# Loading the first image pair by one transfer and the second by four, in a Winograd-row convolution

## The chip, the core and the metric

The kernel runs on one core of a Trainium2 chip. The metric is the device time of one execution in microseconds. The core has five engines that each run their own instructions in order: TensorE (PE; its weight loads are listed apart as PEld), VectorE (DVE), ScalarE (ACT), GpSimd (POOL) and SyncE (SP). SP, ACT and POOL also issue DMA transfers. In the profile a transfer issued on SP is in queue q1, on ACT in q10, on POOL in q0.

## The reference

A 3x3 convolution with zero padding of one, over 16 images of 64 channels and 64x64 pixels, to 128 channels, all in float32:

```python
x_pad = np.pad(x, ((0, 0), (0, 0), (1, 1), (1, 1)), mode='constant')
for b in range(batch):
    for co in range(c_out):
        for ci in range(c_in):
            for kh in range(3):
                for kw in range(3):
                    output[b, co] += weight[co, ci, kh, kw] * x_pad[b, ci, kh:kh+h, kw:kw+w]
```

The input is 16.8 MB, the output 33.6 MB, the weights 0.3 MB.

## The kernel before

Two images make a pair: their 2 x 64 channels fill the 128 partitions, one row of 64 x 64 pixels in each, so that a pair is a block of 128 consecutive rows of `x_rows`. There are eight pairs (`p` from 0 to 7). A matmul takes 64 partitions, one image; those of the two images (`b2`) follow each other on the two halves of the array.

Pairs of output rows share work. With `s` the sum of the input rows 2j and 2j+1 (tile `ss`), the product of the middle kernel row with `s` (tile U) is common to the even and the odd output row. The even row needs U plus two more kernel-row products (A), the odd row U plus two others (B). That is five kernel-row products for two rows instead of six. The combined weights G21 and G01 are made on POOL (lines 86 and 87), after TensorE has turned the weights (line 84) and ScalarE has copied them out (line 85).

A pair is worked in four blocks of eight row pairs. In each block TensorE runs 6 matmuls for U, 12 for A and 12 for B; ScalarE copies U from PSUM to SBUF (`ut`, line 155); VectorE adds it to A (line 164) and to B (line 167) into the output tiles `ots`. PSUM holds eight tiles. A block takes six, so that the A of the next block finds a free one only when the copies of line 155 have freed U's. After the last block of a pair the first image's output goes out on SP's queue (line 171), the second's on ACT's (line 172 puts it in `held`, line 161 issues it in the next block). The last pair's outputs go out in halves.

Pairs 2 to 7 are loaded by POOL (line 58), each by one transfer that casts float32 to float16 on the way. Pairs 2, 3 and 4 are issued at the start, behind line 87; pairs 5 to 7 wait until a buffer of `xpool` is free. Pairs 0 and 1 come as float32 over SP's queue, into two buffers of the output pool, and are cast on the chip:

- line 42: the weights, 288 KB
- lines 45 and 46: pair 0 (`x0`) in two transfers, rows 0 to 17 of every channel and rows 18 to 63
- line 48: pair 1 (`x1`) in one transfer, all 128 partitions

Pair 0 is then summed by VectorE (line 91) and cast by ScalarE (line 92) in four pieces each, the casts by `cuts` at rows 18, 34 and 50. Each piece waits for the transfers that bring its rows. Pair 1 is summed by POOL in two pieces (line 105) and cast by ScalarE in four, two in the third block of pair 0 and two in the fourth (line 159). `keep` holds instructions in the order in which they are written.

Of the kernel before, what the change touches and what calls it, by code (L numbers as in the profile page):

```python
# [13 lines left out]
def kernel(  # L14
# [6 lines left out]
    nc = tc.nc  # L21
# [7 lines left out]
    x_rows = x.rearrange("b c h w -> (b c) h w")  # L29
# [12 lines left out]
    nc.sync.dma_start(w_raw, w_flat)  # L42
    x0 = opool.tile([128, H, W], F32, tag="ot", name="x0")
    cuts = [(0, 18), (18, 34), (34, 50), (50, 64)]
    for lo, hi in ((0, 18), (18, 64)):
        nc.sync.dma_start(x0[:, lo:hi, :], x_rows[0:128, lo:hi, :])  # L46
    x1 = opool.tile([128, H, W], F32, tag="ot", name="x1")
    nc.sync.dma_start(x1, x_rows[128:256, :, :])
    ident = const.tile([128, 128], F16)
    make_identity(nc, ident)  # L50
    w16 = const.tile([CO, CI * 9], F16)
# [50 lines left out]
    for p in range(NP):  # L102
# [8 lines left out]
        for blk in range(4):  # L111
# [57 lines left out]
            if blk in parts:  # L169
                lo, hi = parts[blk]  # L170
# [34 lines left out]
```

## Time and profile before

| | us |
|---|---|
| median of 3 runs (126.14 to 127.47) | 126.81 |
| the profiled execution | 126.72 |
| its span | 124.9 |
| TensorE busy | 106.7 |
| VectorE busy | 82.6 |
| ScalarE busy | 44.4 |
| POOL busy | 36.9 |
| mean of all DMA, GB/s | 356 |

The span is the stretch of the execution that the profile's clock covers; the time of an execution is some 1.8 us longer. TensorE's busy time is modelled, so a high share of it is not yet a proof that it bounds the kernel. The rows by slice cut the span into 40 parts of 3.1 us and give a digit of busy tenths for each. The DMA row is the mean over 16 DMA engines. The DMA rate counts bytes as they are written, so that a transfer that casts to half the size shows half the rate of what it reads. A number of microseconds "to landing" runs from the issue of a transfer to its completion signal.

The order of the first 24 us, from the timeline: the weights land at 3.4, rows 0 to 17 of pair 0 at 5.9, the first matmul of the convolution starts at 6.59, the other rows land at 9.5, pair 1 lands at 16.9, the matmuls of pair 1 begin at 22.36, and the first store is issued at 23.12.

### The profile page before, as it was taken

The page shows a single profiled execution, that of the slowest core. Times are in us where ns is not written, and L with a number is a line of the kernel's source. Part 1 is how long each engine was busy: PE and PEld are TensorE (multiplying, and loading weights), DVE is VectorE, ACT ScalarE, POOL GpSimd, SP SyncE. Part 2 cuts the span into 40 slices and gives each one's busy share as a digit, 9 for nine tenths or more (in the row PEclk, how much of TensorE's full clock was granted, in tenths as well). Part 3 has the DMA queues.
Part 4 walks back from the last instruction along what each step waited for, and adds up shares of the span by engine and source line. Part 5 has one row for each costly group of instructions (what it writes and reads, how often), then busy time and mean ns, then how long its engine had stood idle before and what let it go on. Part 6 is the DMA issues. An engine that isn't in the chain of part 4 may idle for free.

```text
span 124.9 us, 2407 instructions
## 1 busy us (share of the span) xinstructions
PE 106.7 (85%) x978; PEld 55.9 (45%) x978; DVE 82.6 (66%) x132; ACT 44.4 (36%) x76; POOL 36.9 (30%) x29
## 2 busy tenths in 40 slices
PE   0489999999999999999999999999999999990000
PEld 0334455555555555555555555555555555540000
DVE  0106897877787778788788878777877787772000
ACT  4439569633333333333333333333333333330000
POOL 2391059997059001760008500093000000000000
PEclk9999999999999999999999999999999999999755
DMA  4999999999999999999999999999999999999991
GB/s 127 341 429 409 289 220 220 210 254 357 386 344 354 328 375 359 367 338 344 386 359 354 338 344 401 428 435 441 414 430 430 425 420 435 435 420 407 430 391 66
DMA packets 4042, 44.48 MB, mean 356 GB/s; under 512 B 448, under 2 KB 448, under 8 KB 704
## 3 DMA queue, kind: packets, MB, share of 16 engines
q1 hardware_dynamic: 1872, 21.27, 41.2%
q10 hardware_dynamic: 1296, 16.78, 31.7%
q0 software_dynamic: 864, 6.29, 24.4%
q8 instruction: 7, 0.11, 0.3%
q14 instruction: 3, 0.02, 0.0%
HBM read 17.07 MB, written 33.55 MB: 405 GB/s over the span
## 4 chain that ended last, share of the span: by engine, by line
PE 78%; DMA 6%; ACT 3%; DVE 1%; SPq 1%; issue 1%; DVEq 0%
PE acc L141 78%; DMA x<-in_x_dram 6%; ACT xs L92 2%; ACT ut L155 1%; DVE ot L164 1%; DVE ot L167 0%; DVEq L200 0%; SPq L46 0%; SPq L42 0%; DVEq L164 0%
## 5 line engine op out<-in xcount | busy, mean ns | idle before, releaser
L141 PE MATMUL acc<-xs,Wt 64*128 64x504 f16 (+3 forms) x768 | 94.8, 378 | 0.2
L141 PEld LDWEIGHTS <-Wt 64*128 64x128 f16 x960 | 54.7, 96 | 51.6 <-issue 4.2
L155 ACT COPY ut<-acc 128x512 f32<-128x512 f32 x64 | 34.3, 589 | 60.3 <-issue 40.6
L164 DVE TENSOR_TENSOR ot<-acc,ut 128x512 f32<-128x512 f32 x64 | 41.2, 686 | 21.9 <-PE acc L141 18.0
L167 DVE TENSOR_TENSOR ot<-acc,ut 128x512 f32<-128x512 f32 x64 | 41.1, 684 | 0.0
L141 PE MATMUL acc<-ss,Wt 64*128 64x504 f16 (+1 forms) x192 | 32.5, 384 | 1.0 <-DVE ss L67 1.0
L67 POOL TENSOR_TENSOR ss<-xs 128x1024 f16<-128x1024 f16 x12 | 25.2, 2126 | 23.6 <-DMA xs<-in_x_dram 12.5
L67 DVE TENSOR_TENSOR ss<-x 128x512 f16<-128x512 f32 x4 | 2.6, 689 | 8.8 <-DMA x<-in_x_dram 8.8
L58 POOL DMA_DIRECT2D xs<-in_x_dram x6 | 3.5, 578 | 13.3 <-PE acc L141 13.3
L67 POOL TENSOR_TENSOR ss<-x 128x1024 f16<-128x1024 f32 x2 | 4.7, 2360 | 7.1 <-DMA x<-in_x_dram 7.1
L84 PE MATMUL wp<-ident,w 128*64 128x128 f16 x18 | 1.3, 328 | 4.3 <-POOL w L52 4.3
L92 ACT CAST xs<-x 128x1024 f16<-128x1024 f32 (+2 forms) x4 | 4.0, 1048 | 2.3 <-DMA x<-in_x_dram 2.3
L159 ACT CAST xs<-x 128x1024 f16<-128x1024 f32 x4 | 4.0, 1058 | 0.0
L84 PEld LDWEIGHTS <-w 128*64 128x64 f16 x18 | 1.1, 210 | 4.2 <-POOL w L52 4.2
L85 ACT CAST Wt<-wp 128x384 f16<-128x384 f32 x3 | 1.2, 487 | 2.9 <-PE wp L84 2.9
L86 POOL TENSOR_TENSOR Wt<-Wt 128x384 f16<-128x384 f16 x1 | 1.5, 1460 | 1.7 <-ACT Wt L85 1.7
L85 ACT ACT_TABLE_LOAD x1 | 1.3, 1283 | 0.7 <-PEq L189 0.7
L52 POOL CAST w<-w_raw 128x576 f16<-128x576 f32 x1 | 0.7, 663 | 2.2 <-DMA w_raw<-in_weight_dram 2.2
L87 POOL TENSOR_TENSOR Wt<-Wt 128x384 f16<-128x384 f16 x1 | 0.9, 902 | 0.0
masks.py:199 POOL TENSOR_SCALAR_AFFINE_SELECT ident<-ident 128x128 f16<-128x128 f16 x1 | 0.3, 292 | 0.1
masks.py:197 POOL MEMSET ident<- 128x128 f16 x1 | 0.2, 205 | 0.3 <-POOLq L189 0.3
L189 POOL MEMSET const-float32-0.0<- 128x1 f32 x1 | 0.1, 98 | 0.2 <-issue 0.2
(3 smaller groups left out, 0.3 us busy)
## 6 DMA issues: line engine op xcount, KB each, us to landing
out_dram<-ot SPq DMA_DIRECT2D x7, 2048.0 KB, 20.1
out_dram<-ot ACTq DMA_DIRECT2D x7, 2048.0 KB, 19.8
xs<-in_x_dram POOLq DMA_DIRECT2D x6, 1024.0 KB, 25.9
x<-in_x_dram SPq DMA_DIRECT2D x1, 2048.0 KB, 14.8
out_dram<-ot SPq DMA_DIRECT2D x2, 1024.0 KB, 11.6
out_dram<-ot ACTq DMA_DIRECT2D x2, 1024.0 KB, 11.5
x<-in_x_dram SPq DMA_DIRECT2D x1, 1472.0 KB, 7.9
x<-in_x_dram SPq DMA_DIRECT2D x1, 576.0 KB, 4.7
```

The costliest lines, as they stand in the source:

```text
L58: keep(nc.gpsimd.dma_start(xs[p], x_rows[128 * p : 128 * p + 128, :, :]))
L67: eng.tensor_add(ss[p][:, lo : lo + n, :], v[:, lo : lo + n, 0, :], v[:, lo : lo + n, 1, :])
L84: nc.tensor.matmul(wp[q : q + 64, k * CO : k * CO + CO], w16[:, t::9], ident)
L85: keep(nc.scalar.copy(wrow(g), wp[:, 0 : 3 * CO]))
L86: keep(nc.gpsimd.tensor_sub(wrow(G21), wrow(G2), wrow(G1)))
L87: keep(nc.gpsimd.tensor_sub(wrow(G01), wrow(G0), wrow(G1)))
L92: keep(nc.scalar.copy(xs[0][:, lo:hi, :], x0[:, lo:hi, :]))
L141: nc.tensor.matmul(tiles[b2][:, lo - j0 : hi - j0, c_lo:c_hi], Wt[p0 : p0 + 64, wi, kw, :], rhs, start=i == 0, stop=i == n - 1,)
L155: keep(nc.scalar.copy(ut, U[b2]))
L159: keep(nc.scalar.copy(xs[1][:, lo : lo + 16, :], x1[:, lo : lo + 16, :]))
L164: nc.vector.tensor_add(ots[b2][:, j0 : j0 + RB, 0, :], A[b2], us[b2])
L167: nc.vector.tensor_add(ots[b2][:, j0 : j0 + RB, 1, :], Bt[b2], us[b2])
```

## The change

Pair 0 is loaded by one transfer of all 64 rows in place of two. Pair 1 is loaded by four transfers of 32 partitions each, of all rows, in place of one. Order on the queue, tiles, and everything that reads them stay as they are; a reader of `x0` now waits for the one transfer, a reader of all partitions of `x1` for four.

```diff
     cuts = [(0, 18), (18, 34), (34, 50), (50, 64)]
-    for lo, hi in ((0, 18), (18, 64)):
-        nc.sync.dma_start(x0[:, lo:hi, :], x_rows[0:128, lo:hi, :])
+    nc.sync.dma_start(x0, x_rows[0:128, :, :])
     x1 = opool.tile([128, H, W], F32, tag="ot", name="x1")
-    nc.sync.dma_start(x1, x_rows[128:256, :, :])
+    for c in range(0, 128, 32):
+        nc.sync.dma_start(x1[c : c + 32, :, :], x_rows[128 + c : 160 + c, :, :])
```

## The prediction, made before the changed kernel ran

> **What bounds the kernel now.** I read the page first: the rows by slice, the DMA queues and the chain.
>
> ```profile
> span 124.9 us, 2407 instructions
> ...
> PEclk9999999999999999999999999999999999999755
> DMA  4999999999999999999999999999999999999991
> ...
> q1 hardware_dynamic: 1872, 21.27, 41.2%
> q10 hardware_dynamic: 1296, 16.78, 31.7%
> q0 software_dynamic: 864, 6.29, 24.4%
> ...
> PE 78%; DMA 6%; ACT 3%; DVE 1%; SPq 1%; issue 1%; DVEq 0%
> ```
>
> The chain says TensorE, 78%. But it ends at the last tensor_add, at 113.3 us, and the span goes on to 124.9: the last 11 us are stores that drain. The three queues' shares add to 97.3% and the DMA row is full from slice 2 to slice 39. So there are two lines side by side: TensorE's from the first matmul on, and a DMA line without a hole. A delay on the first reaches the end only if it makes a hole in the second; work added to the second reaches the end by itself.
>
> Next, the chain in order of time, for what the first pair's load holds up.
>
> ```profile
> 1.63 7.86 DMA x<-in_x_dram
> 9.49 0.02 issue
> 9.51 2.83 ACT xs L92 x3
> 12.34 0.98 ACT ut L155 x2
> 13.32 0.04 issue
> 13.36 97.40 PE acc L141 x882
> ```
>
> Today's path into steady state is not the first matmul (6.59) but rows 18 to 63 of x0: they land at 9.49, ScalarE casts three pieces (2.83), then copies the first U out of PSUM (0.98). In TensorE's weight-load row of the timeline the wait shows as 12.88 to 13.37, 0.49 us.
>
> Last, stretches (start:end, length, busy us of PE, PEld, DVE, ACT, POOL, then clock, DMA share, GB/s) and the DMA issues.
>
> ```profile
> 3.00:4.00 1.00, 0.00 (x0) 0.00 (x0) 0.00 (x0) 0.00 (x0) 0.47 (x1) 1.00 1.00 283
> ...
> 9.00:12.00 3.00, 3.00 (x22) 1.33 (x20) 1.90 (x3) 2.49 (x3) 0.88 (x2) 1.00 1.01 429
> 20.00:24.00 4.00, 4.00 (x42) 2.11 (x38) 2.97 (x5) 3.80 (x6) 4.00 (x3) 1.00 1.02 213
> 100.00:110.00 10.00, 10.00 (x98) 5.28 (x94) 7.95 (x13) 3.57 (x7) 0.00 (x0) 1.00 1.01 431
> ```
> ```profile
> x<-in_x_dram SPq DMA_DIRECT2D x1, 2048.0 KB, 14.8
> ...
> x<-in_x_dram SPq DMA_DIRECT2D x1, 1472.0 KB, 7.9
> x<-in_x_dram SPq DMA_DIRECT2D x1, 576.0 KB, 4.7
> ```
>
> A busy DMA moves 429 GB/s where descriptors are large, 283 where x0's first 18 rows travel, and fills SBUF at 213 where the loads of line 58 cast to half the bytes.
>
> **First pair, one transfer.** The packet records of the trace hold 128 descriptors for each transfer of x. Those of 4608 bytes took 280 ns on average, those of 11776 took 448, those of 16384 took 611. Sixteen engines share them: today 128 x (280 + 448) / 16 = 5.82 us, as one transfer 128 x 611 / 16 = 4.89. The DMA line loses 0.9 us of work. If the slowness of the small ones came from being the first to move and not from their size, it loses nothing: 0 to 0.9. All 64 rows then land between 9.49 - 0.9 = 8.6 and 9.5. One issue of 0.42 us leaves SP's queue.
>
> What this does to TensorE: the first DVE sum waits for rows 0 to 17, which landed at 5.85 (1.16 issued, 4.7 to land); the first matmul came 0.74 later. The same 0.74 after 8.6 to 9.5 gives a first matmul at 9.3 to 10.2, so 2.75 to 3.65 later. From the landing ScalarE has all four casts to do (1.17 + 2.83) and two copies (0.98), 5.0 us; TensorE itself reaches the point where it waited today 0.74 + 6.3 = 7.0 us after the landing. So the 0.49 us wait goes, and TensorE's own work is late next: a shift of 2.26 to 3.16 for everything behind it. Two bounds more. TensorE's weight loads come every 0.43 us from 6.98 to 11.09 and about twice as fast afterwards, although the granted clock says 1.00: it starts slow. That slow stretch is 4.5 us from the first matmul and 6.8 from the transposes at 4.25; starting its count anew could cost (6.8 - 4.5) / 2 = 1.15 more, while a step at a fixed 11.1 us would leave only 1 to 1.8 us of it and give back about 1.4. The shift is 0.9 to 4.3, 2.7 as the value.
>
> How much of it the end sees is read from the stores. Those of the sixth pair were issued at 87.2 and 87.8, and the answer for that stretch reads:
>
> ```profile
> out_dram<-ot SPq DMA_DIRECT2D x1, 2048.0 KB, 17.0
> out_dram<-ot ACTq DMA_DIRECT2D x1, 2048.0 KB, 16.5
> ```
>
> They land at 104.2; with 0.5 us from last packet to landing (as x0: 8.99 and 9.49) DMA has work until 103.7. The next stores are issued at 99.97, and a packet follows 1.0 us (w_raw) to 1.8 us (this store) after its issue: 101.0 to 101.8. The margin is 1.9 to 2.7 us, 2.3 as the value, the smallest at any of the stores: the last ones, 112.78 and 113.37, land 10.9 and 10.6 later though 2 MB at 429 need 4.9. So TensorE's shift of 2.7 alone costs 0.4, and nothing if DMA has more work than today: then the line has no hole.
>
> **Second pair, four transfers of 32 channels.** The same bytes in the same 128 descriptors of 16384, behind x0 on the same queue. SP issues three more at 0.43 us and is done about 3.4 instead of 2.5; the next thing on SP is a store at 23.12, and x1's packets start at 8.4, so this is hidden. POOL's sum (line 67) and ScalarE's cast (line 159) wait on four semaphores for one; the waiting instructions seen on queues take 17 ns each.
>
> The open price is how fast a transfer that lies on a quarter of the partitions moves: every transfer of this trace spans all 128. Lowest: as x1 today, 611 ns, nothing added. (A gain is excluded: 429 GB/s is what every large transfer here gets.) Highest: the slowest that a load fills SBUF here, 213 GB/s, so 2.10 MB in 9.8 us instead of 4.9, +4.9. The row nearest by size is x0's first piece, 576 KB beside these 512: its 4608 bytes at 611/16384 would be 172 ns and took 280, 1.63 times as long. By that ratio x1 costs 4.89 x 0.63 = +3.1, and I take it; both ends stay for the range. It is DMA work, while DMA is full, so nothing hides it.
>
> [...]
>
> Who waits if x1 lands late? At +2.2 (3.1 less 0.9) it lands at 19.1. ScalarE reaches the cast of x1 at 17.61 + 2.26 = 19.9, no wait. At +4.9 it stands 1.9 us, and behind it the fourth block's U copy and so PSUM and TensorE; that adds at most 1.9 to TensorE's shift and falls into DMA's larger backlog. POOL's two sums (2.36 each) end by 23.8, the first at 21.5; the second pair's matmuls begin at 22.36 + 2.26 = 24.6.
>
> **Sum.** DMA work +3.1 - 0.9 = +2.2; TensorE's shift 2.7 is under the margin then, 2.3 + 2.2. The profiled execution took 126.72 (1.8 beside its span), 0.09 under the median of 126.81: 126.72 + 2.2 = 128.9.
>
> **Rivals and chances.** Forecast, 0.62: the quarter transfers are slower, 1.5 to 4.9; with 0 to 0.9 saved, 127.3 to 131.6, likeliest 128.9. For it: the full DMA row. Against: the descriptors are x1's own.
>
> Second, 0.20: the quarters cost nothing, and TensorE's late start makes a hole before the seventh pair's stores. The shift of 2.26 to 4.3 less the margin of 1.9 to 2.7 is 0 to 2.4: 126.7 to 129.1, middle 127.1. For it: the chain. Against: each store but that one has a larger margin.
>
> Third, 0.18, not slower: the quarters cost nothing, and x0's saved work reaches the end. It decides at the margin: with 0.9 less work the margin is 1.4, so the shift must be under 1.4. It is if TensorE speeds up at a fixed time (0.9 to 1.8). Then 126.72 - 0.9 = 125.8; with a shift of 2.3 it is 126.7. Against: the two small descriptors may have been slow for being first.
>
> A difference under 1% (1.27 us) can't be told from none. Slower by more: 0.57 of the first and 0.10 of the second, 0.67. Same: 0.05, 0.10 and 0.13, 0.28. Faster: 0.05, the third with the ramp better than its row. The range 126.1 to 131.0 leaves out some 0.08 at each end.
>
> **What would show it.** x0's single landing at 8.6 to 9.5 and a first matmul 0.74 behind; no 0.49 us gap before the second block's weight loads. x1's packets at 700 to 1200 ns instead of 611, GB/s under 300 around 9 to 12 us, x1's last landing after 18. The DMA row still full up to the drain and the last add 2 to 4 us later, with the last stores landing in about as much or more than 10.6. I am wrong if x1's packets stay at 611, or if the DMA row has holes at 26 or 102 us; then the margin sets the time.

## The result and the profile after

The changed kernel takes 129.71 us at the median of six executions, the kernel before 126.73: a ratio of 1.0239 with a 95% interval of 1.0211 to 1.0267. It is slower by 3.0 us. The profiled execution took 129.72 us with a span of 127.9.

The page of the changed kernel, in the rows that answer to those of before:

```profile
span 127.9 us, 2415 instructions
...
DMA  5999999999999999999999999999999999999992
...
q1 hardware_dynamic: 1776, 21.27, 43.5%
q10 hardware_dynamic: 1296, 16.78, 30.9%
q0 software_dynamic: 864, 6.29, 23.5%
...
PE 81%; DMA 6%; DVE 2%; issue 1%; DVEq 0%; SPq 0%
```

The bytes of each queue are the same, and the DMA row is as full as before over a span 3.0 us longer. Of the three shares only that of q1, SP's queue, has grown, although the span by which it is divided has grown too: 41.2% of 124.9 was 51.5 us of all sixteen engines, 43.5% of 127.9 is 55.6.

The chain of waits in order of time (start, length, what) shows how TensorE starts now:

```profile
1.17 7.93 DMA x<-in_x_dram
9.10 0.02 issue
9.12 0.70 DVE ss L67
9.83 0.04 issue
9.87 104.24 PE acc L141 x948
```

All of x0 lands at 9.10. VectorE's first sum follows, and the first matmul of the convolution starts at 9.87 in place of 6.59. ScalarE's casts, which stood between x0 and the steady state before, are no longer on the chain, and TensorE then goes without a break to 114.11, 3.35 us later than before.

The stretches (start:end, length, busy us of PE, PEld, DVE, ACT, POOL, clock, DMA share, GB/s) show what happens to x1, whose packets begin at 7.9:

```profile
9.00:12.00 3.00, 2.13 (x12) 0.87 (x13) 2.50 (x4) 2.88 (x3) 0.52 (x1) 1.00 1.02 208
...
100.00:110.00 10.00, 10.00 (x96) 5.14 (x94) 7.97 (x14) 3.62 (x7) 0.00 (x0) 1.00 1.01 428
```

From 9 to 12 us x1 moves all but alone, in both kernels. The DMA engines are as busy as they were, 1.02 for 1.01, and move 208 GB/s where they moved 429. Late in the run the rate is 428, for 431 before. The packet records of the trace (one record for each descriptor) give the same in another unit: x1's 128 descriptors of 16384 bytes took 614 ns on average before and 1156 ns now. 128 x (1156 - 614) / 16 engines is 4.3 us more work on a DMA line that was already full.

### The profile page after: what moved, and what is told of

Its sections match the earlier page's. It is cut to its first block, busy times and chain, and to the rows that moved or that the text cites. A ratio compares the mean times of both kernels' runs of the same rounds, so it can differ in the third digit from the quotient of the medians.

```text
span 127.9 us, 2415 instructions
## 1 busy us (share of the span) xinstructions
PE 106.7 (83%) x978; PEld 54.5 (43%) x978; DVE 82.9 (65%) x132; ACT 44.5 (35%) x76; POOL 36.3 (28%) x29
## 3 DMA queue, kind: packets, MB, share of 16 engines
q1 hardware_dynamic: 1776, 21.27, 43.5%
## 4 chain that ended last, share of the span: by engine, by line
PE 81%; DMA 6%; DVE 2%; issue 1%; DVEq 0%; SPq 0%
PE acc L141 81%; DMA x<-in_x_dram 6%; DVE ot L164 1%; DVE ss L67 1%; DVE ot L167 0%; DVEq L200 0%; SPq L42 0%; DVEq L164 0%
## 5 line engine op out<-in xcount | busy, mean ns | idle before, releaser
L141 PE MATMUL acc<-xs,Wt 64*128 64x504 f16 (+3 forms) x768 | 89.6, 380 | 0.0
L141 PEld LDWEIGHTS <-Wt 64*128 64x128 f16 x960 | 53.4, 96 | 55.9 <-issue 7.4
L164 DVE TENSOR_TENSOR ot<-acc,ut 128x512 f32<-128x512 f32 x64 | 41.2, 686 | 23.7 <-PE acc L141 21.4
L167 DVE TENSOR_TENSOR ot<-acc,ut 128x512 f32<-128x512 f32 x64 | 41.2, 685 | 0.9 <-PE acc L141 0.9
L141 PE MATMUL acc<-ss,Wt 64*128 64x504 f16 (+1 forms) x192 | 27.0, 384 | 4.1 <-DVE ss L67 4.1
L86 POOL TENSOR_TENSOR Wt<-Wt 128x384 f16<-128x384 f16 x1 | 0.9, 907 | 1.7 <-ACT Wt L85 1.7
L87 POOL TENSOR_TENSOR Wt<-Wt 128x384 f16<-128x384 f16 x1 | 0.9, 907 | 0.0
```

What stands on the lines that cost most here:

```text
L86: keep(nc.gpsimd.tensor_sub(wrow(G21), wrow(G2), wrow(G1)))
L87: keep(nc.gpsimd.tensor_sub(wrow(G01), wrow(G0), wrow(G1)))
L141: nc.tensor.matmul(tiles[b2][:, lo - j0 : hi - j0, c_lo:c_hi], Wt[p0 : p0 + 64, wi, kw, :], rhs, start=i == 0, stop=i == n - 1,)
L164: nc.vector.tensor_add(ots[b2][:, j0 : j0 + RB, 0, :], A[b2], us[b2])
L167: nc.vector.tensor_add(ots[b2][:, j0 : j0 + RB, 1, :], Bt[b2], us[b2])
```

## The experiments

Two theories were set against each other. D: the span ends when a DMA line without holes has done its work, and TensorE's start counts only when it makes a hole. T: the end moves with TensorE's start. Within D it was open why the four transfers cost so much.

### Each part of the change by itself

The first pair's part alone (a1_x0_one):

```diff
-    for lo, hi in ((0, 18), (18, 64)):
-        nc.sync.dma_start(x0[:, lo:hi, :], x_rows[0:128, lo:hi, :])
+    nc.sync.dma_start(x0, x_rows[0:128, :, :])
```

> Only the first pair's part of the change: x0 by one transfer, x1 by one as before. Theory D (the span ends with the DMA line; TensorE's start counts only beyond its margin of 1.9 to 2.7 us): TensorE's last work comes 2.5 to 3.4 us later than before, the DMA line has 0.5 us less work, and the end moves by 0 to +1.2 us; the last stores land sooner after their issue than before (10.6 us becomes 8 to 9). Theory T (the end moves with TensorE's start): +2.5 to +3.4 us, nearly all of the change's +3.0, and the last stores land 10.6 us after their issue as before.

Measured: ratio 1.0015 (0.9988 to 1.0043), no difference that can be told. Yet TensorE's work ends late. VectorE's last adds, which wait for it, start at 114.78 instead of 112.06, 2.7 us later. First this kernel, then the kernel before (the same line can have another number in each kernel, as the edits add or remove lines):

```profile
114.78 1.28 DVE L166 TENSOR_TENSOR ot<-acc,ut 128x512 f32<-128x512 f32 x2
```

```profile
112.06 1.28 DVE L167 TENSOR_TENSOR ot<-acc,ut 128x512 f32<-128x512 f32 x2
```

A stretch of this kernel shows where the rest of that went:

```profile
101.00:104.00 3.00, 3.00 (x32) 1.57 (x30) 2.42 (x5) 1.07 (x2) 0.00 (x0) 1.00 0.51 213
```

The same stretch of the kernel before:

```profile
101.00:104.00 3.00, 3.00 (x32) 1.59 (x28) 2.52 (x4) 0.94 (x2) 0.00 (x0) 1.00 1.00 421
```

DMA stood idle for half of three microseconds, 1.5 us, just ahead of the seventh pair's stores, the place that the prediction had named; all the other stretches are full. So 1.2 of the 2.7 were swallowed, and 1.5 stood as a hole. Of the hole 0.2 (by the ratio) to 0.8 us (by the profiled span, 124.9 to 125.7) came through to the end: the packets of this kernel took 0.2 us less in all (121.7 to 121.5 us of sixteen engines, here and below without packets of 4 bytes), and the rest is not accounted for. The last stores land sooner, 8.5 and 8.5 us after their issue instead of 10.9 and 10.6. T is out.

The second pair's part alone (a2_x1_quarters):

```diff
-    nc.sync.dma_start(x1, x_rows[128:256, :, :])
+    for c in range(0, 128, 32):
+        nc.sync.dma_start(x1[c : c + 32, :, :], x_rows[128 + c : 160 + c, :, :])
```

> Only the second pair's part: x1 by four transfers of 32 partitions, x0 by two as before. Theory D: x1's packets take 1000 to 1300 ns for 611, the DMA line has 3.5 to 4 us more work, and the end moves by about that, +3 to +4 us, although the first matmul stays at 6.6. Theory T: the first matmul stays at 6.6 and the end moves only by what ScalarE's wait for x1 costs TensorE, 0 to +2 us.

Measured: ratio 1.0348 (1.0308 to 1.0388), 4.4 us, more than the whole change. x1's descriptors took 1274 ns; that is 5.3 us more DMA work, and the span grew by 5.1. Here x1 is also late for its readers. From the timeline, TensorE:

```profile
26.50 1.46 PE L142 MATMUL acc<-ss,Wt 64*128 64x512 f16 x6 [2.81 <-POOL ss L68]
```

and ScalarE:

```profile
24.04 1.99 ACT L160 CAST xs<-x 128x1024 f16<-128x1024 f32 x2 [5.15 <-DMA x<-in_x_dram]
```

TensorE stands 2.81 us before the second pair, and after that wait it starts slow. The granted clock (the column before the DMA share) reads 0.57 from 26 to 28 us:

```profile
26.00:28.00 2.00, 1.50 (x8) 0.64 (x9) 1.45 (x3) 2.00 (x5) 2.00 (x2) 0.57 1.02 213
```

The last adds start at 117.95, 5.9 us late. This run therefore moves both lines and does not by itself separate the theories. Both expected too little, T with 0 to +2 and D with +3 to +4. Why x1's packets are slower here (1274 ns) than in the changed kernel (1156 ns) stays open. It accounts for 0.9 us (128 x 118 / 16) of the 1.6 by which the two parts, 0.2 and 4.4, exceed the whole. The rest fits x0's saving of 0.5 in DMA work, which this run has not, and the 0.2 of a1_x0_one's hole, which the whole has not; that is argued and not shown.

### TensorE late without other transfers, and more transfers without TensorE late

a3_x1_first issues x1 ahead of x0's two pieces:

```diff
+    nc.sync.dma_start(x1, x_rows[128:256, :, :])
     for lo, hi in ((0, 18), (18, 64)):
         nc.sync.dma_start(x0[:, lo:hi, :], x_rows[0:128, lo:hi, :])
-    nc.sync.dma_start(x1, x_rows[128:256, :, :])
```

> The kernel before with x1's transfer issued ahead of x0's two: the same transfers, so the same DMA work, but TensorE starts about 4.9 us later. Theory D: the margin of 1.9 to 2.7 is used up, and the end moves by 4.9 less the margin, +2.2 to +3.0 us, with a hole in the DMA row or stores that land 2 to 3 us sooner after their issue. Theory T: +4.9 us. A theory in which DMA work alone decides: 0.

Measured: ratio 1.0460 (1.0426 to 1.0494), 5.8 us; the span grew by 5.4. This is above the expectation of both theories, because TensorE's steady part starts at 20.86 instead of 13.36: 7.5 us late and not 4.9. The chain shows what it waited for:

```profile
2.10 14.89 DMA x<-in_x_dram
16.99 0.02 issue
17.01 2.83 ACT xs L92 x3
19.84 0.98 ACT ut L155 x2
20.82 0.04 issue
20.86 97.40 PE acc L141 x882
```

The second piece of x0 lands at 16.99 instead of 9.49, which is the whole 7.5; the casts and copies behind it take as long as before. It comes behind x1, and it also meets POOL's first loads, whose packets begin at 12.16: from 12 to 17 us POOL's queue took 75% of the DMA engines' time and SP's 29%. With 7.5 in place of 4.9, D's sum is 7.5 less a margin of 1.9 to 2.7, 4.8 to 5.6, and the span agrees; T would be 7.5. The holes are plain in two stretches, first in this run and then in the kernel before:

```profile
28.00:31.00 3.00, 3.00 (x32) 1.60 (x30) 2.29 (x4) 2.80 (x4) 0.43 (x1) 1.00 0.03 5
106.00:108.00 2.00, 2.00 (x24) 1.03 (x22) 2.00 (x4) 0.61 (x2) 0.00 (x0) 1.00 0.26 107
```

```profile
28.00:31.00 3.00, 3.00 (x32) 1.57 (x29) 2.27 (x5) 1.07 (x2) 2.54 (x2) 1.00 1.03 358
106.00:108.00 2.00, 2.00 (x22) 1.05 (x20) 1.27 (x3) 1.07 (x2) 0.00 (x0) 1.00 1.02 434
```

Before the first store of the first pair, DMA moves next to nothing (share 0.03); before the seventh pair's stores it stands three quarters of two microseconds. The two holes are 4.4 us, and the packets of this run took 1.1 us longer in all (121.7 to 122.8); together that is what the span grew by.

c1_more_bytes adds a load that nothing reads, so as to lengthen the DMA line and nothing else:

```diff
+    again = const.tile([128, H // 2, W], F16)
...
             load(p + 4)
+            if p == 3:
+                nc.gpsimd.dma_start(again, x_rows[0:128, 0:32, :])
```

> The kernel before with one more load that nothing reads, 32 rows of the first pair (1 MB), issued on POOL behind the load of the last pair, at some 49 us: 128 descriptors of 8192 source bytes, at 309 ns each 2.5 us of DMA work. TensorE has no reason to start or run later. Theory D (the end is the DMA line's): +2.0 to +2.7 us with TensorE's last add where it was. Theory T: 0.

Measured: ratio 1.0193 (1.0149 to 1.0236), 2.4 us. But the load was not held in its place in the program and went out at the start, beside x0, so that the last adds started at 116.17, 4.1 us late. D's figure came out, though not its condition that TensorE stays where it was. T would be 0 by its forecast and 4.1 by this start, and neither came. c3_more_bytes_late holds it where it was meant to be:

```diff
-                nc.gpsimd.dma_start(again, x_rows[0:128, 0:32, :])
+                keep(nc.gpsimd.dma_start(again, x_rows[0:128, 0:32, :]))
```

> As c1_more_bytes, but with the extra megabyte held at its place, behind the load of the last pair at some 49 us: in c1_more_bytes it went out at the very start and made TensorE late too. Now TensorE's start is that of the kernel before. Theory D (the end is the DMA line's): 128 x 0.309 / 16 = 2.5 us more DMA work, the end +2.0 to +2.7 us, TensorE's last add still near 113. Theory T (the end moves with TensorE): 0.

Measured: ratio 1.0199 (1.0173 to 1.0225), 2.5 us. The end of its timeline:

```profile
112.06 1.28 DVE L170 TENSOR_TENSOR ot<-acc,ut 128x512 f32<-128x512 f32 x2
112.76 0.33 SPq L98 DMA_DIRECT2D out_dram<-ot  x1
113.36 0.34 ACTq L98 DMA_DIRECT2D out_dram<-ot  x1
```

The last adds start at 112.06, to the hundredth where they start in the kernel before, and the last stores are issued at the same times (112.78 and 113.37 there). They land 13.8 and 13.4 us after their issue instead of 10.9 and 10.6. The end of TensorE's work has not moved, and the kernel is 2.5 us slower by 2.5 us of DMA work (121.7 to 124.2). That is D alone.

### Why a quarter of the partitions costs so much

a4_x1_comb is the changed kernel with four transfers of the same size, each over every fourth partition:

```diff
-    for c in range(0, 128, 32):
-        nc.sync.dma_start(x1[c : c + 32, :, :], x_rows[128 + c : 160 + c, :, :])
+    for c in range(4):
+        nc.sync.dma_start(x1[c::4, :, :], x_rows[128 + c : 256 : 4, :, :])
```

> The changed kernel, but each of x1's four transfers takes every fourth partition (c, c+4, c+8, ...), so that 32 partitions from all over the 128 are written at a time. If the price comes from lying on 32 neighbouring partitions: packets near 611 ns again, the time as a1_x0_one. If it comes from there being four transfers of 512 KB: packets of 1000 to 1300 ns, the time as the changed kernel, +3.0 us.

Measured: ratio 1.0036 (1.0009 to 1.0064), 612 ns a descriptor. Its stretch beside the changed kernel's 208 GB/s:

```profile
9.00:12.00 3.00, 1.64 (x8) 0.66 (x9) 2.39 (x4) 2.39 (x3) 1.61 (x3) 1.00 1.03 437
```

Four transfers of 512 KB cost nothing that could be told from a1_x0_one. What costs is that the 32 rows of a transfer are neighbours. They are neighbours among the partitions, and in all of these runs they are neighbours in DRAM too: the comb takes every fourth row there as well. No run separates the two sides.

b2_x1_halves takes two transfers of 64 neighbours:

```diff
-    for c in range(0, 128, 32):
-        nc.sync.dma_start(x1[c : c + 32, :, :], x_rows[128 + c : 160 + c, :, :])
+    for c in range(0, 128, 64):
+        nc.sync.dma_start(x1[c : c + 64, :, :], x_rows[128 + c : 192 + c, :, :])
```

> The changed kernel with x1 in two transfers of 64 neighbouring partitions instead of four of 32. [...] If the price falls with the share of the partitions that a transfer covers: packets near 611 to 800 ns, 0 to +1.2 us.

Measured: ratio 1.0255 (1.0196 to 1.0314), 3.2 us, 1144 ns a descriptor. From 9 to 12 us:

```profile
9.00:12.00 3.00, 1.96 (x10) 0.83 (x11) 2.50 (x4) 2.70 (x3) 0.43 (x1) 1.00 0.99 202
```

Half of the partitions is as slow as a quarter (208 GB/s): from the one to the other the price does not fall.

d1_x1_order keeps the quarters and changes their order, to see whether the price depends on which quarter follows which:

```diff
-    for c in range(0, 128, 32):
+    for c in (0, 64, 32, 96):
```

> [...]

Measured: ratio 1.0239 (1.0209 to 1.0269), the changed kernel's own, and 1080 ns a descriptor. From 9 to 12 us:

```profile
9.00:12.00 3.00, 2.24 (x12) 0.95 (x13) 2.50 (x4) 2.99 (x4) 0.56 (x2) 1.00 1.00 218
```

The order brings next to nothing: 76 ns of 1156 in the packets, and no gain in time.

The three runs with neighbours stand together: 208, 202 and 218 GB/s against 429 in the kernel before, about half, and the comb moves 437. What it is that neighbours share, on either side, is in no row of these traces. What is shown is that neighbouring rows are slow and spread ones are not.

### A version that might have beaten both

c2_x0_34 cuts x0 at row 34, for larger descriptors:

```diff
-    for lo, hi in ((0, 18), (18, 64)):
+    for lo, hi in ((0, 34), (34, 64)):
```

> The kernel before with x0 cut at row 34 instead of 18, so that its descriptors hold 8704 and 7680 bytes. Theory D: their 128 x (some 325 + 290) / 16 = 4.9 us is 0.7 to 0.9 us less DMA work than before, TensorE's first matmul comes about 1.3 us later but its steady state still starts from the second piece, some 0.5 us sooner: the end moves by -0.4 to -0.9 us. Theory T: 0 to +1.3 us.

Measured: ratio 1.0006 (0.9975 to 1.0037), no difference, so D's -0.4 to -0.9 did not come. The saving at the front is there: x1's packets begin at 7.95 instead of 8.31, and the packets of the weights and of x0 took 0.5 us less. But the whole of the packets' time did not fall (121.8 us for 121.7), because POOL's loads took 645 ns a descriptor for 633, 0.6 us more. Why they did stays open. No kernel of this study beat the kernel before.

## Why the prediction was right, and where it was not

**The bound.** That the end is a full DMA line beside a TensorE line with a small margin is shown by three runs: c3_more_bytes_late (TensorE untouched, +2.5), a1_x0_one (TensorE 2.7 us late, no difference in time) and a3_x1_first (TensorE 7.5 late, the span 5.4 later). Taken from the end of the profiled spans, the margin was 2.0 in a1_x0_one (2.7 late, 0.8 longer) and 2.1 in a3_x1_first, inside the 1.9 to 2.7. Taken at the hole it was only 1.2 in a1_x0_one. A reason can be read from the packets of the kernel before: the seventh pair's first is at 101.8 and the sixth's last ends at 103.8, so the two share the engines for 2 us, and the sixth's work alone would have been done sooner. The prediction took 103.7 as the end of that work. (It also read x0's last packet at 8.99; it ends at 9.19. That makes little difference here.) That a3_x1_first agrees with the margin is in part luck, since 1.1 of its 5.4 are longer packets. The place of the smallest margin, the seventh pair's stores, was right for a1_x0_one; with a larger delay another hole opened at 28 us, which the prediction only named as a sign.

**The first pair.** The landing (9.10, within 8.6 to 9.5), the first matmul (0.77 after the landing for 0.74) and the end of the 0.49 us wait came as forecast. Two terms were mis-sized. The DMA work saved was taken as 0.9 us, from 611 ns for each of x0's descriptors. They took 646: the 15 that start while the weights still move took 823 and the others 623, and the weights' own packets went from 124 to 141. That leaves 0.5, and x1's packets begin 0.4 us sooner. TensorE's shift was taken as 2.7 and was 3.35, inside the bounds of 0.9 to 4.3. The missing 0.6 is the slow stretch of TensorE's start, which the prediction had put into its bounds: the weight loads came in pairs some 0.4 us apart from 9.87 to 15.61, 5.7 us, where they had done so for 4.5 from the first matmul before. In the weight-load row of the timeline of the changed kernel:

```profile
14.78 0.18 PEld L141 LDWEIGHTS <-Wt 64*128 64x128 f16 x2 [0.25 <-issue]
15.21 0.18 PEld L141 LDWEIGHTS <-Wt 64*128 64x128 f16 x2 [0.25 <-issue]
15.61 1.41 PEld L141 LDWEIGHTS <-Wt 64*128 64x128 f16 x14 [0.23 <-issue]
```

Pairs some 0.4 us apart up to 15.61, and then fourteen in 1.41. The granted clock did change there, against the prediction's reading of 1.00: the trace's first clock record, of 1.00, begins at 15.58 here and at 11.13 in the kernel before, and ahead of the first record the column shows 1.00 for want of one. In a2_x1_quarters, where there is a record, the same pace stands beside 0.57. From the first matmul to the first record of 1.00 it was 5.3 us in c3_more_bytes_late, which starts as the kernel before does (4.5), 2.9 in a4_x1_comb and d1_x1_order, which start near the changed kernel (5.7), and 6.0 in b2_x1_halves. So the change does not set this length, and the 0.6 looks like chance; no run was made for it. None of the 3.35 reached the end: the DMA row has no hole from 100 to 110 us in the changed kernel.

**The second pair.** That the quarters cost DMA work and that nothing hides it was right; the term was too small: +3.1 was taken, between 0 and +4.9, and x1 took 4.3 more. The step that failed is the choice of the nearest row by size, x0's first piece of 576 KB. Size had nothing to do with it: a4_x1_comb moves the same 512 KB at full pace, 437 GB/s. Nor was that row's 280 ns all size: behind x1, in a3_x1_first, the same descriptors took 233. The far end of the range, the rate of 213 GB/s, came out nearest to the 208, and that is luck: it belongs to loads that write half of what they read, and their packets take 633 ns, for the 614 of x1 before. x1's packets at 700 to 1200 ns (1156) and under 300 GB/s at 9 to 12 us came as said. ScalarE did not wait, as said: it reaches its cast at 20.92, as x1 lands. POOL's first sum of x1 ends at 23.3, ahead of the second pair's matmuls at 25.5. In a2_x1_quarters, where TensorE starts early and x1 is later still, ScalarE and TensorE did wait.

**The sum.** 4.3 more for x1 and 0.5 less for x0 and the weights is +3.8; the other queues' packets took 0.5 less, and all packets together take 3.4 us more (121.7 to 125.1). Those of 4 bytes, left out of these figures, took 0.4 more besides. The time moved by 3.0. The forecast of +2.2 fell short by 0.8, for an x1 that was 1.2 dearer and an x0 that saved 0.4 less, with 0.8 of both given back. Of the rivals, the second (no price for the quarters, a hole before the seventh pair's stores) is what a1_x0_one and a4_x1_comb are: 1.0015 and 1.0036, at the low end of its 0 to 2.4 us.

## What to carry to other kernels

Where the DMA row is full to the end, price every edit in DMA engine time first, and let a compute engine's delay count only beyond the work that its stores still find queued (here 2.5 us of added work cost 2.5, in c3_more_bytes_late, and 2.7 us of delay made no difference that can be told, in a1_x0_one): last packet of the stores before, less first packet of the next, and less again where the two overlap. A transfer that is cut as x1 was should still take partitions and rows from all over the 128, every fourth for one, which moved 437 GB/s here; 32 or 64 neighbours moved at half the rate, 202 to 218, in both sizes and both orders that were run. And a transfer's price is read from a row that shares its cause. Of the two rows used here neither did: the one of like size missed by 1.2 us, and the one that came near did so by luck.

## What the hardware did unexpectedly

VectorE's sum of two float32 pieces took 0.69 us in the kernel before and 3.87 in a3_x1_first. There POOL was running its two sums of x1, which in the other kernels come later:

```profile
10.95 3.87 DVE L67 TENSOR_TENSOR ss<-x 128x512 f16<-128x512 f32 x1 [10.95 <-DMA x<-in_x_dram]
```

and POOL in the same run:

```profile
9.60 4.65 POOL L67 TENSOR_TENSOR ss<-x 128x1024 f16<-128x1024 f32 x2
```

POOL is done at 14.25, VectorE at 14.82, 0.57 later: it looks as if VectorE waited inside its instruction for POOL to end. If so it waited for both sums, although POOL's second begins at 11.91 and VectorE's instruction at 10.95. This delayed the first matmul of that run (14.87) but not its steady part, which waited for x0. It goes the other way too: POOL's first weight subtraction (line 86) takes 1.46 us in the kernel before, where it starts together with VectorE's first sum, and 0.91 in the changed kernel, where VectorE is idle. The adds of lines 164 and 167, which read PSUM, keep their 0.68 beside POOL's sums. No run was made for this alone.

POOL's loads, issued at 7.8 to 8.2 us, put their first packet on the engines only at 11.96 in the kernel before and at 14.61 in the changed one, when x1 had started 92 and 96 of its 128 descriptors. That is no rule: in a4_x1_comb x1 had started 119. What holds them back stays open.
